# Inverse of the 32x32 diagonal blocks in the second mixer: one partition per block, or four partitions per block and a transposition on TensorE

## The chip, the cores and the metric

The kernel runs on one core of a Trainium2 chip. The metric is device time in microseconds (us). Before the change the median of three runs is 1167.81 us, from 1162.26 to 1176.41.

## The reference: what is computed

Two blocks of a language model run one after the other on 256 tokens of width 1024. The first has a stick-breaking attention, an RWKV-7 recurrence and a feed-forward layer. The second has a token mixer (a gated delta rule and HGRN2, four heads of 128 each) and a mixture of 64 experts. This case is about one line of the gated delta rule:

```python
L = jnp.where(strict, jnp.einsum('bhncd,bhnsd->bhncs', kb, kc) * decay, 0.0)
sol = lax.linalg.triangular_solve(L + jnp.eye(CHUNK, dtype=L.dtype), rhs,
                                  left_side=True, lower=True, unit_diagonal=True)
```

The kernel works on chunks of 128 tokens and not of 64, so there are 4 heads times 2 chunks = 8 systems of 128x128, all unit lower triangular. It forms the inverse of I + L for each. What the later products take is N, the transposed inverse.

## The kernel before

The kernel is one stream of instructions for each engine. Its parts are Python generators that are stepped in the order of a string. For the second mixer this string is `MIXER` ('kkkffkfkkfkfffffffkfqkkqqqqqqqqddghh...'): k is `proj_gdn` (keys, gates, the matrices L and the inverse), f is `proj_hgrn`, q is `proj_qv` (the query and value projections with a convolution and a SiLU), g is `proj_gates2`, d is `gdn` (the products that read N) and h is `hgrn`. The string gives priorities only: a planner in the framework, with its own costs for each instruction, then orders the instructions of each engine, so instructions of f, q, g and h stand between those of the inverse. On the chip each engine's queue runs in that order.

**Projections.** Weights arrive as units of 8 tiles of 128x128 (512 KB). `unit` loads `raw` from DRAM by the SP queue (L274), ScalarE rounds it to `whi` (L324), and VectorE, or for a fixed list of units GpSimd, takes the rest `wlo` = raw - whi (L325). There are three buffers each of raw, whi and wlo. Each tile is then multiplied in three TensorE matmuls (L330, L331, L332, or L352, L357, L358 for the gates): whi by the high part of the input, whi by its low part, wlo by the high part.

**The inverse** (`inverse`, called in the second mixer for 8 systems, and in the first block for 16 systems with `extra`, before the change the same code). Each 128x128 system has four 32x32 blocks on its diagonal, so 8 systems give 32 small blocks. L goes to DRAM (L421) and comes back with one block in each partition, 32 partitions in use (L424, four DMAs). `base_inverse` inverts all of them at once by forward substitution: for each of 31 columns j one VectorE multiplication (L403) and one subtraction (L404) on a rectangle of 31-j rows by j+1 columns. ScalarE writes the transposed copy (L405). Both forms go to DRAM (L435, two DMAs) and are read back to where they stand on the diagonal: the transposed form into N (L439, four DMAs), the untransposed form of the first three blocks into Mc (L442, three DMAs). Two levels of small TensorE products (`mm` at L413, evacuated at L454, L459, L464, L473 and L477) then fill 64x64 and 128x128. `gdn` reads N.

Around the inverse on VectorE stand the convolutions of q (L1145), its SiLU (L1150), the gates (L1314) and the levels of HGRN2 (L1435, L1436, L1438, L1447); on GpSimd its share of L325, L1439 and copies (L1425); on TensorE the products of HGRN2 (L1441) and the transpositions (`tr`, L389). After the mixer come the output projection, the router, a sort of the experts, and the experts, whose weights stream in at full DMA rate.

Of the kernel before, what the change touches and what calls it, by code (L numbers as in the profile page):

```python
# [10 lines left out]
F32 = mybir.dt.float32  # L11
# [3 lines left out]
AF = mybir.ActivationFunctionType  # L15
OP = mybir.AluOpType
# [193 lines left out]
class Ker:  # L210
# [193 lines left out]
            nc.vector.tensor_tensor(M[:, c:, :c], M[:, c:, :c], u, op=OP.subtract)  # L404
        nc.scalar.activation(MT[:P], M.rearrange("p a b -> p b a"), AF.Copy)  # L405

    def inverse(self, L, ns, N, tag, extra=None):

        nc = self.nc
        mm = lambda out, l, r: nc.tensor.matmul(out, l, r, start=True, stop=True)  # L413
        ne = 4 * ns + (8 if extra else 0)
        nc.gpsimd.memset(N, 0.0)
        work = self.alloc("gate", [4, 1024])
        Mc = work[:, 0, :ns * 64].rearrange("p (a b) -> p a b", b=64)
        nc.gpsimd.memset(Mc, 0.0)
        inst, A0, A1 = (work[:, i].rearrange("p (a b) -> p a b", b=32) for i in (1, 2, 3))
        dl = self.dram.tile([128, ns, 128], F32, name=f"dl{ns}")  # L420
        nc.sync.dma_start(dl, L)  # L421
        for k in range(4):
            q = slice(32 * k, 32 * k + 32)
            nc.sync.dma_start(inst[k * ns:(k + 1) * ns], dl[q, :, q].rearrange("t s c -> s t c"))  # L424
        if extra:
            dm = self.dram.tile([128, 2, 32], F32, name="dm")
            nc.sync.dma_start(dm, extra[0])
            for g in range(2):
                o = 4 * ns + 4 * g
                nc.sync.dma_start(inst[o:o + 4], dm[:, g].rearrange("(i t) c -> i t c", i=4))  # L430
        A = A0, A1
        self.base_inverse(inst, A0, A1, ne)
        da = self.dram.tile([2, ne, 32, 32], F32, name=f"da{ns}")
        for x in range(2):
            nc.sync.dma_start(da[x], A[x][:ne])  # L435
        for k in range(4):
            q = slice(32 * k, 32 * k + 32)
            s = slice(k * ns, (k + 1) * ns)
            nc.sync.dma_start(N[q, :, q], da[1, s].rearrange("s t c -> t s c"))  # L439
            if k < 3:  # L440
                o = 32 * (k % 2)
                nc.sync.dma_start(Mc[q, :, o:o + 32], da[0, s].rearrange("s t c -> t s c"))  # L442
            if extra:
                nc.sync.dma_start(extra[1][q, :, q], da[1, 4 * ns:].rearrange("(g i) t c -> i t g c", g=2)[k])
        yield

        X = work[:, 1, :ns * 64].rearrange("p (a b) -> p a b", b=64)
        half = [(slice(64 * p, 64 * p + 32), slice(64 * p + 32, 64 * p + 64)) for p in range(2)]
        v = lambda p: p.rearrange("p (a b) -> p a b", b=32)[:, :ns]
        px = [v(self.psum(tag)) for _ in range(2)]  # L450
        for p, (f, z) in enumerate(half):
            for s in range(ns):
                mm(px[p][f, s], L[z, s, f], N[z, s, z])
            nc.scalar.activation(X[f, :, :32], px[p][f], AF.Copy)  # L454
        pn = [v(self.psum(tag)) for _ in range(2)]
        for p, (f, z) in enumerate(half):
            for s in range(ns):
                mm(pn[p][f, s], Mc[f, s, :32], X[f, s, :32])
            nc.vector.tensor_scalar(N[f, :, z], pn[p][f], -1.0, None, op0=OP.mult)  # L459
        pm = v(self.psum(tag))  # L460
        f, z = half[0]
        for s in range(ns):
            mm(pm[z, s], X[f, s, :32], Mc[f, s, :32])
        nc.scalar.activation(Mc[z, :, :32], pm[z], AF.Copy, scale=-1.0)  # L464
        yield

        X = work[:, 2, :ns * 64].rearrange("p (a b) -> p a b", b=64)
        f, z = slice(0, 64), slice(64, 128)
        for b in range(0, ns, 8):
            px = self.psum(tag).rearrange("p (a b) -> p a b", b=64)  # L470
            for s in range(8):
                mm(px[f, s], L[z, b + s, f], N[z, b + s, z])
            nc.scalar.activation(X[f, b:b + 8], px[f], AF.Copy)  # L473
            pn = self.psum(tag).rearrange("p (a b) -> p a b", b=64)
            for s in range(8):
                mm(pn[f, s], Mc[f, b + s], X[f, b + s])
            nc.vector.tensor_scalar(N[f, b:b + 8, z], pn[f], -1.0, None, op0=OP.mult)  # L477
# [1714 lines left out]
```

## Time and profile before

| | |
|---|---|
| median of 3 runs | 1167.81 us (1162.26 to 1176.41) |
| the profiled execution, its own time | 1168.17 us |
| its span, first to last instruction | 1166.3 us |
| mean granted clock of TensorE, share of full speed | 0.971 |
| TensorE matmul busy | 1085.4 us (93%) |
| VectorE busy | 682.4 us (59%) |
| ScalarE busy | 436.3 us (37%) |
| GpSimd busy | 243.7 us (21%) |
| DMA, mean over the span | 249 GB/s |

The profiled execution is 0.36 us above the median. Engines in the rows: PE is TensorE's matmuls, PEld its weight loads, DVE is VectorE, ACT is ScalarE, POOL is GpSimd, SP is the engine whose queue issues most DMAs (SPq). A row of the timeline has the start in us, the duration in us, engine, line, operation, output<-inputs, partitions x elements, count, and in brackets the idle time just before with what ended it. The inverse of the second mixer takes from 588.8 us (L goes to DRAM) to about 674 us.

### The profile page before, as it was taken

How to read it: one execution, taken by the hardware profiler on the slowest of the kernel's cores; microseconds unless marked ns; L12 is line 12 of the kernel's file. 1: busy time of each engine (PE TensorE's matmuls, PEld its weight loads, DVE VectorE, ACT ScalarE, POOL GpSimd, SP SyncE). 2: the span in 40 equal slices, each digit the busy share in tenths (PEclk: the TensorE clock that was granted, in tenths of full speed). 3: DMA queues.
4: the chain of work that ended last, by engine and by line, in shares of the span. 5: the costliest groups of instructions: out<-in, count | busy, mean ns of one | idle time of the engine just before them, and what ended most of it. 6: DMA issues, size and time to landing. Idle time of an engine off the chain costs nothing.

```text
span 1166.3 us, 20384 instructions
## 1 busy us (share of the span) xinstructions
PE 1085.4 (93%) x8050; PEld 825.3 (71%) x8050; DVE 682.4 (59%) x1211; ACT 436.3 (37%) x707; POOL 243.7 (21%) x245
## 2 busy tenths in 40 slices
PE   4989899999999999888988999899999999999994
PEld 4889787789989999887988889773454455444441
DVE  5598633356688887878799887612333333333333
ACT  5744433365454444335864635311111111111112
POOL 1251102123321000577462141410000000000000
PEclk9899979999999999999999999799999999999997
DMA  4445511024568988763443405959999999999992
GB/s 171 146 141 178 175 62 38 1 91 163 181 248 288 330 319 326 277 247 136 157 135 126 160 28 187 412 179 373 418 409 418 418 419 419 399 420 418 419 419 115
DMA packets 67496, 290.70 MB, mean 249 GB/s; under 512 B 15984, under 2 KB 17136, under 8 KB 46912
## 3 DMA queue, kind: packets, MB, share of 16 engines
q1 hardware_dynamic: 66528, 287.93, 64.9%
q8 instruction: 66, 1.08, 0.4%
q10 hardware_dynamic: 864, 1.38, 0.3%
q14 instruction: 38, 0.31, 0.1%
HBM read 285.77 MB, written 3.51 MB: 248 GB/s over the span
## 4 chain that ended last, share of the span: by engine, by line
PE 51%; DVE 13%; DMA 9%; issue 4%; ACT 4%; POOL 3%; SPq 0%; DVEq 0%; POOLq 0%; ACTq 0%
PE bank L1892 14%; PE bank L1920 7%; DMA wada<-in_W_ada_dram 5%; PE acc L1789 4%; PE bank L1852 4%; DMA er<-in_E_dram 3%; DVE wlo L325 3%; DVE wada L1098 2%; PE p_b L797 2%; PE p_b L357 2%; PE p_b L358 2%; ACT k L306 2%; PE p_b L352 2%; PE p_b L331 2%; PE p_b L332 2%
## 5 line engine op out<-in xcount | busy, mean ns | idle before, releaser
L324 ACT ACTIVATE whi<-raw 128x1024 fp32r<-128x1024 f32 x168 | 175.4, 1055 | 100.9 <-DMA raw<-in_W_dram 36.9
L325 DVE TENSOR_TENSOR wlo<-raw,whi 128x1024 fp32r<-128x1024 f32 x138 | 179.3, 1305 | 54.9 <-ACT whi L324 50.6
L358 PE MATMUL p_b<-k,wlo 128*128 128x256 f32 x608 | 173.5, 286 | 6.9 <-DVE wlo L325 5.1
L357 PE MATMUL p_b<-k,whi 128*128 128x256 f32 x608 | 173.1, 285 | 2.3 <-DVE k L325 2.3
L352 PE MATMUL p_b<-k,whi 128*128 128x256 f32 x608 | 172.8, 285 | 1.5 <-ACT whi L324 0.7
L332 PE MATMUL p_b<-k,wlo 128*128 128x256 f32 (+2 forms) x496 | 144.1, 295 | 12.9 <-DVE wlo L325 8.9
L330 PE MATMUL p_b<-k,whi 128*128 128x256 f32 (+2 forms) x496 | 146.4, 299 | 6.7 <-ACT k L324 4.1
L331 PE MATMUL p_b<-k,whi 128*128 128x256 f32 (+2 forms) x432 | 126.8, 296 | 1.5 <-DVE k L1122 0.9
L358 PEld LDWEIGHTS p_b<-k,wlo 128*128 128x128 f32 x608 | 115.7, 191 | 11.0 <-DVE wlo L325 6.9
L325 POOL TENSOR_TENSOR wlo<-raw,whi 128x1024 fp32r<-128x1024 f32 x30 | 80.9, 2700 | 191.0 <-ACT whi L324 159.1
L357 PEld LDWEIGHTS p_b<-k,whi 128*128 128x128 f32 x608 | 115.7, 190 | 3.7 <-DVE k L325 2.7
L352 PEld LDWEIGHTS p_b<-k,whi 128*128 128x128 f32 x608 | 115.5, 190 | 3.1 <-ACT whi L324 0.9
L332 PEld LDWEIGHTS p_b<-k,wlo 128*128 128x128 f32 (+1 forms) x496 | 96.4, 196 | 15.6 <-DVE wlo L325 10.9
L330 PEld LDWEIGHTS p_b<-k,whi 128*128 128x128 f32 (+1 forms) x496 | 96.8, 197 | 12.4 <-ACT k L324 5.1
L1892 PE MATMUL bank<-er,x 128*32 128x512 f32 (+2 forms) x464 | 91.9, 611 | 2.7 <-DMA er<-in_E_dram 2.5
L1920 PE MATMUL bank<-er,k 128*32 128x512 f32 (+2 forms) x488 | 90.2, 604 | 2.6 <-DMA er<-in_E_dram 1.4
L1098 DVE SCALAR_TENSOR_TENSOR wada<-wada,crow 128x1024 f32<-128x1024 f32 x48 | 74.9, 1564 | 22.9 <-DMA wada<-in_W_ada_dram 22.8
L1892 PE MATMUL bank<-er,h 128*32 128x512 f32 (+2 forms) x488 | 87.3, 595 | 0.0
L1840 POOL TENSOR_TENSOR k<-k,masks 128x128 f32<-128x128 f32 (+3 forms) x44 | 17.4, 425 | 334.2 <-DVE y L325 309.2
L331 PEld LDWEIGHTS p_b<-k,whi 128*128 128x128 f32 (+1 forms) x432 | 85.5, 199 | 2.2 <-DVE k L1122 1.1
L1897 ACT ACTIVATE k<-bank 128x256 f32<-128x256 f32 x24 | 9.2, 385 | 195.1 <-PE bank L1892 195.1
L1898 DVE SCALAR_TENSOR_TENSOR k<-k,gs,bank 128x256 f32<-128x256 f32 x24 | 11.5, 480 | 101.8 <-ACT k L1897 101.8
(478 smaller groups left out, 2043.8 us busy)
## 6 DMA issues: line engine op xcount, KB each, us to landing
er<-in_E_dram SPq DMA_DIRECT2D x132, 1024.0 KB, 18.0
raw<-in_W_dram SPq DMA_DIRECT2D x168, 512.0 KB, 3.9
wada<-in_W_ada_dram SPq DMA_DIRECT2D x48, 512.0 KB, 5.4
xa<-in_E_dram SPq DMA_DIRECT2D x24, 1024.0 KB, 13.2
xa<-in_Sh_dram SPq DMA_DIRECT2D x2, 1024.0 KB, 9.2
k<-in_xT_dram SPq DMA_DIRECT2D x4, 272.0 KB, 5.0
dl<-x SPq DMA_DIRECT2D x1, 1024.0 KB
x<-in_xT_dram SPq DMA_DIRECT2D x1, 1024.0 KB
```

What stands on the lines that cost most here:

```text
L324: ins = self.nc.scalar.activation(hi, src, AF.Copy)
L325: (engine or self.nc.vector).tensor_tensor(lo, src, hi.bitcast(F32), op=OP.subtract)
L330: mm(out, w[0], x[0], start=start, stop=False)
L331: mm(out, w[0], x[1], start=False, stop=False)
L332: mm(out, w[1], x[0], start=False, stop=stop)
L352: a = mm(p[:, i], w[0], v[0], start=(n == 0), stop=False, **kw)
L357: mm(p[:, i], w[0], v[1], start=False, stop=False, **kw)
L358: mm(p[:, i], w[1], v[0], start=False, stop=last, **kw)
L1098: nc.vector.scalar_tensor_tensor(w, w, 1.0, c, op0=OP.mult, op1=OP.mult, accum_out=self.mod[:, o:o + 1])
L1789: self.nc.tensor.matmul(self.acc[t], w, x, start=t not in self.started, stop=False, skip_group_check=True)
L1892: mm(ph[t], X[:, k, i * 128 + t.start:i * 128 + t.stop], u[:, kk * 512:kk * 512 + 512], start=(k == 0), stop=(k == KD - 1), skip_group_che ...
L1920: nc.tensor.matmul(py[t], q.H[:, k, t], u[:, k * 1024 + c * 512:k * 1024 + c * 512 + 512], start=(k == 0), stop=(k == 1), skip_group_check ...
```

## The change

For the call without `extra` (the second mixer) the blocks are inverted by a new function `by_columns`; the first block keeps the code of before under the name `by_blocks`. A block now goes to four partitions, 128 in all: partition 32c + 8k + s holds block k of system s and solves for columns c, c+4, c+8, ... of its inverse. To load it takes 16 DMAs in place of four, since each block is copied four times. A step j works on 31-j rows by j//4+1 columns. Five small memsets on GpSimd set up the unit columns, in place of two. Only the transposed form goes through DRAM: one DMA out, in runs of 128 B, and four back into N. The three DMAs into Mc are gone; after the `yield`, TensorE transposes all eight 128x128 systems of N and six ScalarE copies take the first three diagonal blocks into Mc. The levels above stay as they are.

```diff
+    def by_columns(self, L, N, Mc, work, tag):
+        nc = self.nc
+        ns = 8
+        b = lambda x, n: x.rearrange("p (a b) -> p a b", b=n)
+        inst, M, MT = b(work[:, 1], 32), b(work[:, 2, :256], 8), b(work[:, 3, :256], 32)
+        u, flat = work[:, 2, 256:512], work[:, 2, :256]
+        nc.gpsimd.memset(flat, 0.0)
+        for c in range(4):
+            nc.gpsimd.memset(flat[32 * c:32 * c + 32, 8 * c::33], 1.0)
+        dl = self.dram.tile([128, ns, 128], F32, name=f"dl{ns}")
+        nc.sync.dma_start(dl, L)
+        for k in range(4):
+            q = slice(32 * k, 32 * k + 32)
+            for c in range(4):
+                o = 32 * c + ns * k
+                nc.sync.dma_start(inst[o:o + ns], dl[q, :, q].rearrange("t s c -> s t c"))
+        for j in range(31):
+            r, c = 31 - j, j // 4 + 1
+            v = u[:, :r * c].rearrange("p (a b) -> p a b", b=c)
+            nc.vector.tensor_tensor(v, inst[:, j + 1:, j:j + 1].to_broadcast([128, r, c]), M[:, j:j + 1, :c].to_broadcast([128, r, c]), op=OP.mult)
+            nc.vector.tensor_tensor(M[:, j + 1:, :c], M[:, j + 1:, :c], v, op=OP.subtract)
+        nc.scalar.activation(MT, M.rearrange("p a b -> p b a"), AF.Copy)
+        da = self.dram.tile([8, 128, 32], F32, name=f"da{ns}")
+        nc.sync.dma_start(da.rearrange("i p t -> p i t"), MT)
+        back = da.rearrange("i (c k s) t -> (i c) k s t", c=4, k=4)
+        for k in range(4):
+            q = slice(32 * k, 32 * k + 32)
+            nc.sync.dma_start(N[q, :, q], back[:, k])
+        yield
+        for h in (0, 4):
+            pt = b(self.psum(tag), 128)
+            for s in range(4):
+                self.tr(pt[:, s], N[:, h + s])
+            for k in range(3):
+                q = slice(32 * k, 32 * k + 32)
+                o = 32 * (k % 2)
+                nc.scalar.activation(Mc[q, h:h + 4, o:o + 32], pt[q, :, q], AF.Copy)
+
...
+    def inverse(self, L, ns, N, tag, extra=None):
...
+        if not extra:
+            yield from self.by_columns(L, N, Mc, work, tag)
+        else:
+            yield from self.by_blocks(L, ns, N, Mc, work, extra)
```

## Rows read from the trace of the kernel before

**Rows 1.** The page, part 2: busy tenths in 40 slices

```profile
PE   4989899999999999888988999899999999999994
...
DVE  5598633356688887878799887612333333333333
```

**Rows 2.** Stretches: length, busy (count) of PE, PEld, DVE, ACT, POOL; PEclk, DMA share, GB/s

```profile
597.00:652.10 55.10, 46.78 (x359) 45.40 (x358) 54.50 (x109) 28.16 (x38) 15.22 (x10) 0.94 0.37 128
600.30:604.20 3.90, 3.84 (x20) 3.84 (x20) 3.66 (x9) 1.68 (x3) 2.81 (x5) 0.57 0.36 134
616.40:622.00 5.60, 5.52 (x32) 5.35 (x32) 5.60 (x10) 1.36 (x2) 2.60 (x1) 0.70 0.54 189
653.20:674.00 20.80, 20.80 (x226) 18.62 (x227) 15.92 (x22) 13.88 (x21) 7.19 (x5) 1.00 0.42 129
674.00:690.00 16.00, 13.79 (x109) 12.33 (x108) 15.06 (x29) 4.29 (x8) 4.37 (x6) 1.00 0.10 34
```

**Rows 3.** Timeline of TensorE: four idle times in 597:653

```profile
600.36 0.38 PE L332 MATMUL p_b<-k,wlo 128*128 128x256 f32 x1 [2.34 <-POOL wlo L325]
...
616.48 0.39 PE L332 MATMUL p_b<-k,wlo 128*128 128x256 f32 x1 [2.49 <-DVE wlo L325]
...
631.73 0.39 PE L332 MATMUL p_b<-k,wlo 128*128 128x256 f32 x1 [1.64 <-POOL wlo L325]
...
648.80 0.38 PE L358 MATMUL p_b<-k,wlo 128*128 128x256 f32 x1 [1.66 <-DVE wlo L325]
```

**Rows 4.** VectorE groups, 597 to 652.1 us: the base inverse

```profile
L404 DVE TENSOR_TENSOR gate<-gate,kt 32x31 f32<-32x31 f32 (+15 forms) x31 | 18.8, 606 | 0.2
...
L403 DVE TENSOR_TENSOR kt<-gate 32x31 f32<-32x31 f32 (+15 forms) x31 | 10.9, 352 | 0.3
```

**Rows 5.** Timelines of VectorE and GpSimd: one overlap, durations by shape

```profile
605.28 2.50 DVE L404 TENSOR_TENSOR gate<-gate,kt 32x156 f32<-32x156 f32 x1
...
604.87 2.75 POOL L325 TENSOR_TENSOR wlo<-raw,whi 128x1024 fp32r<-128x1024 f32 x1 [1.76 <-ACT whi L324]
...
597.34 0.19 DVE L403 TENSOR_TENSOR kt<-gate 32x31 f32<-32x31 f32 x1
...
648.68 0.23 DVE L403 TENSOR_TENSOR kt<-gate 32x87 f32<-32x87 f32 x1
...
623.22 0.40 DVE L403 TENSOR_TENSOR kt<-gate 32x256 f32<-32x256 f32 x1
...
594.54 0.41 DVE L1435 TENSOR_TENSOR h<-h 128x256 f32<-128x256 f32 x1
```

**Rows 6.** SP's queue at the inverse's start, landing of block loads

```profile
591.42 1.54 SPq L424 DMA_DIRECT2D gate<-dl  x4
...
593.05 0.94 SPq L274 DMA_DIRECT2D raw<-in_W_dram  x2
...
DMA to landing us min/median/max: 4.4/4.9/5.1
```

**Rows 7.** Timelines of ScalarE and VectorE: the first later weight splits

```profile
602.80 2.98 ACT L324 ACTIVATE whi<-raw 128x1024 fp32r<-128x1024 f32 x3
...
604.15 1.20 DVE L325 TENSOR_TENSOR wlo<-raw,whi 128x1024 fp32r<-128x1024 f32 x1
```

**Rows 8.** The way back: SP, ScalarE, TensorE; transpositions in 560:735

```profile
652.04 2.81 SPq L435 DMA_DIRECT2D da<-gate  x2
...
652.50 2.01 ACT L405 ACTIVATE gate<-gate 32x1024 f32<-32x1024 f32 x1
...
666.46 0.38 ACT L454 ACTIVATE gate<-p_b 32x256 f32<-32x256 f32 x1
...
661.97 0.69 PE L413 MATMUL p_b<-k,k 32*32 32x32 f32 x16
...
L389 PE MATMUL p_b<-masks,k 128*128 128x128 f32 x26 | 4.2, 280 | 2.1 <-DVE k L1188 0.8 <-DVE k L1337 0.8 <-DVE k L374 0.5
```

**Rows 9.** SP's waits from 690 us: us, times, longest

```profile
SPq L1804 <- DVE masks L1709: 15.4, 1, 15.4
```

More of the change, by code (lines that the diff above doesn't have):

```diff
@@ L405, in base_inverse @@
         nc.scalar.activation(MT[:P], M.rearrange("p a b -> p b a"), AF.Copy)
-    def inverse(self, L, ns, N, tag, extra=None):
+    def by_columns(self, L, N, Mc, work, tag):
         nc = self.nc
[L413 to L418, printed above, removed]
+        ns = 8
[33 more added lines that the diff above has]
+                nc.scalar.activation(Mc[q, h:h + 4, o:o + 32], pt[q, :, q], AF.Copy)
@@ L419, in inverse, with by_blocks @@
+    def by_blocks(self, L, ns, N, Mc, work, extra):
+        nc = self.nc
+        ne = 4 * ns + 8
         inst, A0, A1 = (work[:, i].rearrange("p (a b) -> p a b", b=32) for i in (1, 2, 3))
@@ L424, in inverse @@
             nc.sync.dma_start(inst[k * ns:(k + 1) * ns], dl[q, :, q].rearrange("t s c -> s t c"))
[L425 to L430, printed above, removed]
+        dm = self.dram.tile([128, 2, 32], F32, name="dm")
+        nc.sync.dma_start(dm, extra[0])
+        for g in range(2):
+            o = 4 * ns + 4 * g
+            nc.sync.dma_start(inst[o:o + 4], dm[:, g].rearrange("(i t) c -> i t c", i=4))
         A = A0, A1
@@ L442, in inverse @@
                 nc.sync.dma_start(Mc[q, :, o:o + 32], da[0, s].rearrange("s t c -> t s c"))
-            if extra:
-                nc.sync.dma_start(extra[1][q, :, q], da[1, 4 * ns:].rearrange("(g i) t c -> i t g c", g=2)[k])
+            nc.sync.dma_start(extra[1][q, :, q], da[1, 4 * ns:].rearrange("(g i) t c -> i t g c", g=2)[k])
         yield
+    def inverse(self, L, ns, N, tag, extra=None):
+        nc = self.nc
+        mm = lambda out, l, r: nc.tensor.matmul(out, l, r, start=True, stop=True)
+        nc.gpsimd.memset(N, 0.0)
+        work = self.alloc("gate", [4, 1024])
+        Mc = work[:, 0, :ns * 64].rearrange("p (a b) -> p a b", b=64)
+        nc.gpsimd.memset(Mc, 0.0)
+        if not extra:
+            yield from self.by_columns(L, N, Mc, work, tag)
+        else:
+            yield from self.by_blocks(L, ns, N, Mc, work, extra)
         X = work[:, 1, :ns * 64].rearrange("p (a b) -> p a b", b=64)
```

## The prediction, made before the changed kernel ran

> **What bounds the kernel now.** I read the page first, by slices: TensorE is busy nine tenths or more in most of them, and VectorE reaches its highest shares, eight tenths and more, only in the middle [rows 1]. Then the stretches: from 597 to 652.1 us, the time in which the second mixer's base inverse runs, VectorE is busy for 54.5 of 55.1 us, and TensorE for 46.8 [rows 2]. So here, and only here, VectorE is the full engine and TensorE the one that waits. From 653.2 to 674 us TensorE is busy throughout, and from 674 to 690 us for 13.8 of 16 us [rows 2]. The idle times of TensorE come next: four long ones of 2.34, 2.49, 1.64 and 1.66 us, all for a `wlo` (L325), twice one made on GpSimd [rows 3]. They make 8.1 of the 8.3 us that TensorE stands idle in the stretch. After two of them the granted clock is down: its mean is 0.57 over 3.9 us and 0.70 over 5.6 us [rows 2], between the levels of 2.4 and 1.2 GHz. That costs 3.9 x 0.43 = 1.7 us and 5.6 x 0.30 = 1.7 us. All that TensorE loses beside the inverse is thus 8.3 + 3.4 = 11.7 us, about 1% of the kernel. Nothing that the change does to VectorE there can give back more, unless it also shortens the work after it.
>
> A gain here passes on to the end. The loads of the sorted experts wait 15.4 us for the sort (L1709), which follows the mixer and the router [rows 9], so they move with the mixer's end.
>
> **VectorE, the term that is meant to fall.** L403 and L404 have the same 31 shapes, but take 10.9 and 18.8 us [rows 4]. The 7.9 us between them are not arithmetic: the L404 at 605.28 us takes 2.50 us while GpSimd's L325 runs from 604.87 to 607.62 us [rows 5], and there are four such pairs. Twice 10.9 = 21.8 us is then the plain time of the 62 instructions.
>
> The new 62 instructions work on 8 to 76 elements in a partition, 1560/31 = 50 in the mean, where the old ones had 31 to 256. A row of 31 elements takes 0.19 us, one of 87 0.23 us, one of 256 0.40 us, and 256 elements in 128 partitions take 0.41 us [rows 5], so more partitions cost nothing. At 50 elements I take 0.20 us: 62 x 0.20 = 12.4 us. The ends are 62 x 0.23 = 14.3 us, and 62 x 0.17 = 10.5 us with the line through 31 and 256 drawn on to 8 elements. The number of instructions stays, so most of what is left is the fixed part. Saved: 21.8 - 12.4 = 9.4 us, between 7.5 and 11.3.
>
> Are the 7.9 us of stalls saved too? The rows show a VectorE instruction with two inputs in SBUF that ends when GpSimd's ends [rows 5]; GpSimd keeps the same splits. I leave the stalls where they are: another L404 or an L325 will meet them. The Trainium skill, SBUF — State Buffer, section SBUF: two separate sides, speaks against the change in the same way: the port pair that VectorE and GpSimd share is an exclusive lock, and whoever comes second blocks fully. By that rule the stall stays and 9.4 us is all; without it up to 17.3 us would go.
>
> **What TensorE gets of it.** VectorE then has 54.5 - 9.4 = 45 us of work in the stretch, TensorE needs 46.8 - 3.4 = 43.4 us. The two are nearly even, and the order on VectorE decides. By idle time: the one before 600.36 us, with its slow stretch (2.34 + 1.7), ends with GpSimd's own work and began before the base inverse did at 597.34 us [rows 3, 5]; it gives nothing. The one before 616.48 us comes when little of the 9.4 us has been saved; I take 1.5 of 2.49 us, and half of the 1.7 us behind it. Those before 631.73 and 648.80 us, late in the stretch, I take in full, 1.64 and 1.66 us. Sum: 1.5 + 0.85 + 1.64 + 1.66 = 5.6 us, between 0 and 2.49 + 1.7 + 1.64 + 1.66 = 7.5 us.
>
> **What is added.**
> - TensorE: 8 transpositions. 26 such take 4.2 us busy, 0.16 us each [rows 8], so 1.3 us on an engine that is full after 653 us. Counted whole.
> - SP's queue: 16 block loads for four. Four took 1.54 us [rows 6], 0.385 us each; twelve more are 4.6 us. Two loads of raw weights stand right behind, at 593.05 us, and move to about 597.7 us; with the 4.4 us that a block load takes to land [rows 6] the first is there at 602.1, and ScalarE takes it up at 602.80 us [rows 7]. That is free with 0.7 us to spare; if the cover is gone it is as much as 4.6 us.
> - The base inverse itself then begins 4.6 us later, at 602 us. Before, VectorE did nothing but base inverse from 597.34 us to the L325 at 604.15 us [rows 5, 7], so a late start idles it where nothing else was ready. The instructions that the planner puts ahead of that L325 have to be caught up. From 0 to 4.6 us; I take 0.4, since some 11 instructions of 0.20 us fit between 602 and 604.2 us.
> - The way back: the second DMA out, the 2.0 us of the old transposed copy and three loads go; one DMA out in short runs, eight transpositions and six copies of about 0.38 us [rows 8] come. Before, the first products came at 661.97 us, 9.9 us after the first DMA out at 652.04 us [rows 8], with TensorE busy on gates and HGRN2. With the base inverse over some 20 us earlier, the same cover (projections of q, gates) is there. Taken as 0; without cover it is a wait on TensorE (below). ScalarE's net is 6 x 0.38 + 0.4 - 2.0 = +0.7 us in a stretch where it is busy for 28.2 of 55.1 us [rows 2]: 0.
> - GpSimd's memsets can run long before, while the work tile is free: 0. The levels above the blocks do not change.
>
> **Sum.** -5.6 + 1.3 + 0.4 = -3.9 us against the profiled execution's 1168.17 us, that is 1164.3, say 1164 us. Its span of 1166.3 us has 1.9 us around it that do not move, and it stands 0.36 us above the median of 1167.81 us. About 1%, 11.7 us, is what a measurement of this kernel can tell from no change; the forecast lies well inside.
>
> **Rivals.**
> - *No change* (1167 to 1170 us): VectorE frees time, but the weight splits wait for GpSimd, ScalarE and raw loads all the same, and 1.3 us of transpositions eat the rest. For it: two of the four idle times end with GpSimd's split [rows 3]. Against: VectorE's 54.5 us of 55.1 [rows 2].
> - *More than forecast*: the inverse is complete some 20 us earlier, so `gdn` can start while projections still run, and the mixer's end packs closer. Then all 11.7 us beside the inverse go, and the 16 - 13.8 = 2.2 us idle from 674 to 690 us [rows 2]: 1168.2 - 13.9 + 1.3 = 1155.6 us. This needs GpSimd's early wait to vanish as well, for which I see no reason, save that the planner's order of all engines is new from 590 us on.
> - *Slower*: the block data arrives late, and instructions that need it stand ahead of work that doesn't, in queues that run in order. At the start: 16 loads at the slower landing of 5.1 us [rows 6], with raw loads behind them, put the base inverse at 603 to 605 us; the L325 at 604.15 us [rows 7] stands behind it and goes late by up to 4.6 us, and TensorE with it, plus a slow stretch of 1.7 us. At the way back: the transpositions stand in TensorE's queue before N has landed. N comes after a DMA out and loads, 9.9 us in all before [rows 8]; if the planner allows for half of that, TensorE stands 5 us and 1.7 us slow. 4.6 + 1.7 + 5 + 1.7 + 1.3 = 14.3 us against a gain of about 3: 1179.5 us. It decides from the point where the round trip is over 4 us longer than planned. The Trainium skill, DMA: Bandwidth & Descriptors, section Specifications, asks for transfers of at least 512 B for line rate; the new DMA out has runs of 128 B into DRAM, and no row here shows such a write. By that rule the way back would be longer and this case likelier.
> - *That VectorE's time does not fall* because the fixed part rules: the 31-element row at 0.19 against 0.40 us [rows 5] leaves no room for that; it is in the ends above.
>
> **Chances.** The forecast (1160 to 1167) 0.43; no change 0.22; more than forecast 0.20, of which 0.13 beyond 1%; slower 0.15, of which 0.10 beyond 1%. So faster by over 1%: 0.13; within: 0.77; slower: 0.10. The range takes in the forecast, no change, and most of both outer cases: 1155 to 1176 us.
>
> **What would show it.** Right: L403 and L404's successors at about 0.20 us apiece, 12 to 14 us with fewer or equal stalls of some 2 us; VectorE below nine tenths beside the inverse; the waits of TensorE for L325 after 610 us shorter; SP's queue holding 16 block loads for about 6 us; first products of the upper levels 15 to 25 us earlier. Wrong: TensorE standing in front of L389 with a DMA as the cause, raw loads that land after ScalarE is free, VectorE idle before the first base instruction with L325 behind it, or a mixer whose later part (674 us on) is stretched by what the first part gained.

## The result, and the profile after

The changed kernel takes 1183.72 us in the median of 11 runs (1178.77 to 1192.26), the kernel before, run beside it, 1169.1 us (1162.26 to 1176.41): a ratio of 1.013, with a 95% interval of 1.0103 to 1.0157. It is 1% slower, where I had forecast 1164 us and a small gain. The profiled execution of the changed kernel took 1192.09 us (span 1190.3), near the upper end of its runs, so I don't compare whole spans: 3.5 us of the difference are there before the change begins (the projections' first product is at 593.2 instead of 589.7 us), and 5 us come behind the router. What the edit can touch directly is the stretch between. I take it from the first product of the projections (the row of TensorE with 1.2 us idle for L1286, L1331 in the changed kernel) to the router's first transposition. It grew from 147.6 to 163.1 us, by 15.5 us, as much as the 1.3% of the timed runs (0.013 x 1169 = 15.2 us). Such a stretch is of one execution, so it shows where the time goes, and the timed runs how much it is.

Cut in three, before: projections; from their last product to the output projection's first (gates, inverse, gated DeltaNet, HGRN2: "the middle" from here on); output projection. Columns as in [rows 2].

```profile
589.74:633.17 43.43, 36.37 (x268) 35.19 (x269) 42.55 (x81) 20.99 (x29) 22.34 (x12) 0.92 0.41 138
633.17:702.93 69.76, 65.17 (x579) 59.57 (x578) 62.45 (x119) 39.10 (x59) 17.29 (x17) 1.00 0.28 94
702.93:737.36 34.43, 32.78 (x258) 31.38 (x258) 20.02 (x40) 14.08 (x27) 5.33 (x8) 1.00 0.68 261
```

The same three in the changed kernel:

```profile
593.22:637.30 44.08, 36.30 (x264) 34.97 (x264) 34.93 (x86) 21.46 (x29) 21.17 (x12) 0.88 0.57 144
637.30:722.26 84.96, 71.22 (x590) 65.49 (x590) 60.23 (x115) 39.48 (x65) 16.65 (x17) 0.94 0.25 74
722.26:756.34 34.08, 32.42 (x255) 31.18 (x255) 19.79 (x39) 14.01 (x27) 5.31 (x8) 1.00 0.70 268
```

Read the second rows: the middle is 15.2 us longer (84.96 - 69.76). TensorE's idle time in it went from 69.76 - 65.17 = 4.6 to 84.96 - 71.22 = 13.7 us, so 9.1 us are waits; its busy time rose by 6.0 us, at a granted clock of 0.94 for 1.00 and with the eight transpositions added. The projections gained nothing: 44.08 for 43.43 us, although VectorE does 7.6 us less there (34.93 for 42.55).

**VectorE did get its time back.** The steps of the base inverse, as groups of the changed kernel between 600 and 650 us; they answer to [rows 4]:

```profile
L428 DVE TENSOR_TENSOR gate<-gate 128x60 f32<-128x60 f32 (+24 forms) x31 | 10.8, 349 | 8.3 <-DMA gate<-dl 7.9
L429 DVE TENSOR_TENSOR gate<-gate 128x60 f32<-128x60 f32 (+24 forms) x31 | 8.7, 281 | 0.5
```

10.8 + 8.7 = 19.5 us for the 29.7 us of L403 and L404: 10.2 us saved, 9.4 forecast. VectorE's timeline shows single steps and a stall; GpSimd's shows what is beside the stall:

```profile
611.70 0.21 DVE L428 TENSOR_TENSOR gate<-gate 128x50 f32<-128x50 f32 x1
611.94 0.21 DVE L429 TENSOR_TENSOR gate<-gate 128x50 f32<-128x50 f32 x1
...
613.20 2.38 DVE L428 TENSOR_TENSOR gate<-gate 128x48 f32<-128x48 f32 x1
```

```profile
612.32 3.19 POOL L325 TENSOR_TENSOR wlo<-raw,whi 128x1024 fp32r<-128x1024 f32 x1 [5.78 <-ACT whi L324]
```

A step of 50 elements takes 0.21 us, and the one that meets GpSimd's split takes 2.38 us: the stall stayed, as forecast. There are three such steps, 7.2 us together, where the kernel before had four, 9.2 us; the other 59 steps take 12.3 us, 0.21 us each. (By the exclusive lock of the Trainium skill, SBUF — State Buffer, section SBUF: two separate sides, this had to be so; the trace agrees, 2.38 for 0.21 us.)

**The start.** SP's queue, VectorE, ScalarE and TensorE of the changed kernel where the base inverse begins; they answer to [rows 3, 6, 7]:

```profile
592.28 0.33 SPq L419 DMA_DIRECT2D dl<-k  x1
594.91 9.53 SPq L424 DMA_DIRECT2D gate<-dl  x16
604.54 1.30 SPq L274 DMA_DIRECT2D raw<-in_W_dram  x3
```

```profile
608.76 0.20 DVE L428 TENSOR_TENSOR gate<-gate 128x31 f32<-128x31 f32 x1 [7.86 <-DMA gate<-dl]
...
609.90 1.06 ACT L324 ACTIVATE whi<-raw 128x1024 fp32r<-128x1024 f32 x1 [3.13 <-DMA raw<-in_W_dram]
...
611.01 0.58 PE L330 MATMUL p_b<-k,whi 128*128 128x256 f32 x1 [2.98 <-ACT whi L324]
...
613.34 0.58 PE L332 MATMUL p_b<-k,wlo 128*128 128x256 f32 x1 [1.11 <-DVE wlo L325]
```

Of these 16 loads, the shortest, the median and the longest on SP, in ns:

```profile
L424 SPq DMA_DIRECT2D gate<-dl x16: 308/369/2006, 594.9 to 603.7; - x16
```

The 16 loads take SP 9.53 us, not the 6.2 us that 16 x 0.385 makes. The base inverse begins 608.76 - 593.22 = 15.5 us behind the projections' first product; before, it was 597.34 - 589.74 = 7.6 us, so it is 7.9 us later, not 4.6. Raw weights stand behind them and are issued at 604.54 us, 12.3 us after the first DMA out; before, with the DMA out at 588.80 us, it was 593.05 - 588.80 = 4.3 us. ScalarE waits for them, TensorE for ScalarE.

**The way back.** SP, then TensorE's first products of the upper levels, as [rows 8]:

```profile
648.14 0.43 SPq L432 DMA_DIRECT2D da<-gate  x1
653.45 1.97 SPq L436 DMA_DIRECT2D k<-da  x4
```

```profile
656.10 0.69 PE L482 MATMUL p_b<-k,k 32*32 32x32 f32 x16 [1.07 <-DMA k<-da]
```

The round trip is 656.10 - 648.14 = 8.0 us, shorter than the 9.9 us before, and TensorE waits 1.07 us at it. But the inverse is not complete some 20 us earlier: counted from the projections' first product, this row is at 656.10 - 593.22 = 62.9 us, before at 661.97 - 589.74 = 72.2 us, 9.3 us earlier. The short steps stand one by one between other work in VectorE's queue, and the last of them ends at 646.2 us. SP stands 5.3 us between the DMA out and the first load. (The Trainium skill, DMA: Bandwidth & Descriptors, section Specifications, asks for 512 B a piece; this DMA out has pieces of 128 B. That it is the size, and not the raw weights that move at the same time, no run here shows; with the longer pieces of the kernel before, such a DMA out landed in 2.4 us at most there, and in up to 5.1 us in e11_before_gates_first.)

**The middle.** This is TensorE's order behind the projections, counted from its instructions: g gates, h HGRN2, i the inverse's upper levels, t transpositions, n norms, d gated DeltaNet, | router weights, m output projection (broken off after 90 of its products). A product counts once here; the trace has two rows for each of h, i, n and d, one for each of the others. First before, then changed:

```
g14 h4 g26 h4 g18 h4 g60 h4 g18 h4 g38 i8 g4 i8 g14 i8 h4 i16 t4 i8 n1 h1 i8 n1 h3 t8 h8 d4 t4 d12 h2 d4 t4 h4 t4 d1
h2 d4 h3 d7 h4 d8 h9 d2 h4 t4 h4 | m3 h8 m18 h4 m69

g48 h16 g39 i8 g9 t8 h1 i8 h4 i24 h3 i8 g6 i8 n2 g8 t4 g26 d4 g13 t4 g2 d4 g6 d8 g9 d4 t4 g4 t4 g1 d1 g5 d4 g6 d7 g6
d8 g4 h4 t4 h4 t4 h8 d2 h8 | h4 | h20 t4 h1 m3 h7 m18 h4 m69
```

Before, the gates are through before gated DeltaNet begins, and HGRN2 and gated DeltaNet take turns. In the changed kernel the last 90 products of the gates come behind gated DeltaNet's norms, 56 of them between its products, HGRN2 has no turn between 663.4 and 694.3 us, and its products then stand almost alone. TensorE there, in the changed kernel:

```profile
694.32 1.05 PE L1486 MATMUL p_b<-h 128*128 128x128 f32 x8
...
697.64 1.13 PE L1490 MATMUL p_b<-h,h 128*128 128x128 f32 x8 [1.83 <-DVE k L1359]
...
705.31 3.36 PE L1486 MATMUL p_b<-h 128*128 128x128 f32 x16 [1.88 <-POOL h L1484]
...
712.59 1.13 PE L1486 MATMUL p_b<-h 128*128 128x128 f32 x8 [0.97 <-DVE h L1483]
715.18 2.11 PE L1486 MATMUL p_b<-h 128*128 128x128 f32 x16 [1.47 <-DVE h L1483]
```

and the corresponding place before, where nothing waits:

```profile
694.78 2.18 PE L1441 MATMUL p_b<-h 128*128 128x128 f32 x18
696.81 1.98 PE L1381 MATMUL p_b<-k,ones 128*128 128x512 f32 x4
698.63 1.05 PE L1445 MATMUL p_b<-h,h 128*128 128x128 f32 x8
```

No level of HGRN2 reads another's product, but each product (L1486, before L1441) needs operands that VectorE, ScalarE and GpSimd make one behind the other (L1480, L1481, the exponential L306, L1483, L1484). With other products between, these steps are hidden; without them TensorE waits. From 694.3 to 722.3 us it waits 8.4 of 28 us. The other 5.3 of its 13.7 us of waits are about as much as the 4.6 us before.

The other part of the 15 us is busy time. Two more waits, and the transpositions:

```profile
639.43 0.35 PE L352 MATMUL p_b<-k,whi 128*128 128x256 f32 x1 [2.14 <-DVE gate L429]
...
657.87 1.04 PE L389 MATMUL p_b<-masks,k 128*128 128x128 f32 x8
...
674.78 1.83 PE L1381 MATMUL p_b<-k,k 128*128 128x128 f32 x8 [1.82 <-DVE k L1205]
```

Behind these two waits, and behind the 1.88 us at 705.31, the granted clock is down. The three spells, then 2 us out of each:

```profile
641.00:645.00 4.00, 4.00 (x23) 4.00 (x23) 4.00 (x13) 1.06 (x1) 0.00 (x0) 0.58 0.65 171
674.00:679.00 5.00, 4.22 (x23) 4.22 (x24) 3.85 (x5) 0.61 (x2) 0.00 (x0) 0.66 0.61 185
705.30:710.00 4.70, 4.69 (x27) 4.69 (x28) 4.04 (x8) 1.89 (x3) 1.54 (x2) 0.64 0.00 0
```

```profile
642.00:644.00 2.00, 2.00 (x11) 2.00 (x11) 2.00 (x7) 0.12 (x1) 0.00 (x0) 0.50 0.84 266
...
676.00:678.00 2.00, 2.00 (x11) 2.00 (x11) 1.88 (x3) 0.00 (x0) 0.00 (x0) 0.50 0.46 123
...
706.00:708.00 2.00, 2.00 (x11) 2.00 (x11) 2.00 (x4) 1.13 (x3) 0.84 (x2) 0.50 0.00 0
```

0.50 is the level of 1.2 GHz, and TensorE does 11 products in 2 us where at 1.00 it does 20 (651 to 653 us). By the means the spells cost 4.00 x 0.42 + 5.00 x 0.34 + 4.70 x 0.36 = 5.1 us, an estimate; with the 1.04 us of the transpositions that is about the 6.0 us of busy time. Before, the middle has no such stretch. Only the third spell stands behind a wait of HGRN2; the first stands behind a wait for a late step of the inverse on VectorE, the second behind the one at gated DeltaNet's first product. So HGRN2's bare end makes 8.4 + 1.7 = 10.1 of the 15.2 us directly.

### The profile page after: what moved, and what is told of

It is laid out like the page before. It is cut to its first block, busy times and chain, and to the rows that moved or that the text cites. A ratio compares the mean times of both kernels' runs of the same rounds, so it can differ in the third digit from the quotient of the medians.

```text
span 1190.3 us, 20429 instructions
## 1 busy us (share of the span) xinstructions
PE 1093.1 (92%) x8058; PEld 834.4 (70%) x8058; DVE 674.5 (57%) x1211; ACT 437.1 (37%) x713; POOL 240.8 (20%) x248
## 4 chain that ended last, share of the span: by engine, by line
PE 51%; DVE 12%; DMA 10%; ACT 3%; POOL 3%; issue 3%; SPq 1%; POOLq 0%; ACTq 0%; DVEq 0%
PE bank L1937 13%; PE bank L1965 7%; DMA wada<-in_W_ada_dram 5%; PE acc L1834 4%; PE bank L1897 4%; DMA er<-in_E_dram 3%; DVE wlo L325 3%; DVE wada L1143 2%; PE p_b L357 2%; PE p_b L358 2%; PE p_b L352 2%; PE p_b L842 2%; ACT k L306 1%; PE bank L1798 1%; PE p_b L332 1%
## 5 line engine op out<-in xcount | busy, mean ns | idle before, releaser
L325 DVE TENSOR_TENSOR wlo<-raw,whi 128x1024 fp32r<-128x1024 f32 x138 | 176.2, 1283 | 58.7 <-ACT whi L324 54.8
L358 PE MATMUL p_b<-k,wlo 128*128 128x256 f32 x608 | 176.0, 290 | 6.5 <-DVE wlo L325 4.7
L352 PE MATMUL p_b<-k,whi 128*128 128x256 f32 x608 | 175.1, 289 | 3.6 <-DVE gate L429 2.1
L357 PE MATMUL p_b<-k,whi 128*128 128x256 f32 x608 | 175.2, 288 | 2.4 <-DVE k L325 2.4
L332 PE MATMUL p_b<-k,wlo 128*128 128x256 f32 (+2 forms) x496 | 144.3, 295 | 10.9 <-DVE wlo L325 7.6
L358 PEld LDWEIGHTS p_b<-k,wlo 128*128 128x128 f32 x608 | 117.9, 194 | 10.2 <-DVE wlo L325 5.9
L352 PEld LDWEIGHTS p_b<-k,whi 128*128 128x128 f32 x608 | 117.3, 193 | 5.7 <-issue 3.5
L357 PEld LDWEIGHTS p_b<-k,whi 128*128 128x128 f32 x608 | 117.8, 194 | 3.9 <-DVE k L325 2.8
L1143 DVE SCALAR_TENSOR_TENSOR wada<-wada,crow 128x1024 f32<-128x1024 f32 x48 | 76.5, 1595 | 21.6 <-DMA wada<-in_W_ada_dram 21.6
```

The source lines that it names most:

```text
L325: (engine or self.nc.vector).tensor_tensor(lo, src, hi.bitcast(F32), op=OP.subtract)
L332: mm(out, w[1], x[0], start=False, stop=stop)
L352: a = mm(p[:, i], w[0], v[0], start=(n == 0), stop=False, **kw)
L357: mm(p[:, i], w[0], v[1], start=False, stop=False, **kw)
L358: mm(p[:, i], w[1], v[0], start=False, stop=last, **kw)
L1143: nc.vector.scalar_tensor_tensor(w, w, 1.0, c, op0=OP.mult, op1=OP.mult, accum_out=self.mod[:, o:o + 1])
```

## The experiments

Theory A: the loss is the order that the planner makes of gates, gated DeltaNet and HGRN2 behind the projections. Theory B, the rival: 16 loads and the way back hold SP's queue, and what needs the data comes late. The stretch is that of the profiled run, one execution of each kernel, with its three parts and TensorE's idle time in the middle:

| run | median us | ratio (95%) | stretch | projections, middle, output | idle in the middle |
|---|---|---|---|---|---|
| before | 1169.1 | 1 | 147.6 | 43.4, 69.8, 34.4 | 4.6 |
| changed | 1183.7 | 1.0130 (1.0103 to 1.0157) | 163.1 | 44.1, 85.0, 34.1 | 13.7 |
| e1_steps | 2774.0, not compared | | 160.3 | 41.7, 84.5, 34.1 | 11.6 |
| e2_turn | 1172.8 | 1.0013 (0.9991 to 1.0035) | 151.3 | 45.8, 71.0, 34.5 | 5.1 |
| e3_pack | 1185.1 | 1.0134 (1.0057 to 1.0211) | 162.8 | 42.8, 85.9, 34.1 | 11.3 |
| e4_order | 1181.7 | 1.0099 (1.0076 to 1.0122) | 156.1 | 43.7, 79.1, 33.3 | 11.8 |
| e5_h_late | 1184.6 | 1.0108 (1.0064 to 1.0152) | 162.3 | 43.4, 84.8, 34.1 | 10.3 |
| e6_h_first | 1191.5 | 1.0178 (1.0120 to 1.0236) | 166.1 | 43.8, 89.6, 32.7 | 15.6 |
| e7_before_h_first | 1187.2 | 1.0135 (1.0081 to 1.0189) | 165.2 | 46.0, 88.3, 31.0 | 14.5 |
| e8_pack_h_first | 1183.1 | 1.0110 (1.0075 to 1.0145) | 163.8 | 43.2, 89.1, 31.5 | 14.3 |
| e9_gates_first | 1179.1 | 1.0157 (1.0044 to 1.0270) | 155.7 | 44.7, 76.5, 34.5 | 8.4 |
| e10_pack_gates_first | 1176.2 | 1.0120 (1.0014 to 1.0226) | 156.9 | 43.0, 79.4, 34.5 | 8.0 |
| e11_before_gates_first | 1176.6 | 1.0140 (1.0025 to 1.0254) | 157.8 | 43.5, 79.3, 35.0 | 10.9 |
| e12_h_in_mix | 1184.6 | 1.0200 (1.0086 to 1.0314) | 161.1 | 42.5, 66.0, 52.6 | 7.1 |

**e1_steps**: the kernel before with the small steps alone; its four loads and its way back stay.

```
-            r, c = B - 1 - j, j + 1
+            r, c = B - 1 - j, j + 1 if P > 32 else j // 4 + 1
...
```

> The kernel before, with the second mixer's 62 base-inverse instructions cut to the sizes of the change (j//4+1 columns, still 32 partitions; the other columns of the blocks are left unsolved); loads, way back and everything else as before. VectorE's relief alone. The planner's order on TensorE is the changed kernel's here: gates spread among the products of gdn, and some 30 products of HGRN2 in a row ahead of the output projection. Theory A (the order: a base inverse that the planner expects earlier pulls gdn ahead and leaves HGRN2's chain bare): 8 to 14 us slower than before, idle times of 1 to 2 us between HGRN2's products. Theory B (the block loads and the way back hold SP's queue): these are as before, so 4 to 9 us faster than before.

Its blocks are left unsolved in part, so the router gets other values and the experts other loads; I read it up to the router. The middle is 84.5 us, as in the changed kernel, without one new DMA. Three parts, by stretches:

```profile
591.77:633.51 41.74, 35.09 (x264) 34.08 (x264) 38.50 (x90) 21.25 (x29) 20.37 (x12) 0.92 0.45 152
633.51:718.04 84.53, 72.96 (x582) 65.95 (x582) 58.85 (x112) 39.46 (x59) 18.62 (x17) 0.90 0.22 73
718.04:752.11 34.07, 32.41 (x254) 31.16 (x254) 19.80 (x39) 14.02 (x27) 5.33 (x8) 1.00 0.72 285
```

and HGRN2's waits at the end are those of the changed kernel, to the hundredth:

```profile
693.07 1.13 PE L1445 MATMUL p_b<-h,h 128*128 128x128 f32 x8 [1.83 <-DVE k L1314]
...
700.73 3.68 PE L1441 MATMUL p_b<-h 128*128 128x128 f32 x16 [1.88 <-POOL h L1439]
708.01 1.13 PE L1441 MATMUL p_b<-h 128*128 128x128 f32 x8 [0.97 <-DVE h L1438]
710.60 3.29 PE L1441 MATMUL p_b<-h 128*128 128x128 f32 x16 [1.47 <-DVE h L1438]
```

TensorE's order there is that of the changed kernel too: again the last 90 products of the gates come behind gated DeltaNet's norms, and HGRN2's stand at the end. So shorter steps are enough for the loss in the middle; theory B is not needed for it. The shares differ: 7.0 us more idle time than before, and 7.8 us more busy time at a clock of 0.90. In the projections this run is 1.7 us shorter than before. The kernel before had 43.4 to 46.0 us there under other orders (e5, e7, e11), so 1 to 2 us in this part can't be told from what an order does.

**e2_turn**: the kernel before with the transposed form made by TensorE (8 transpositions, 6 copies), and its second DMA out and three loads gone.

```
...
-            if k < 3:
+            if k < 3 and extra:
...
+        for h in () if extra else (0, 4):
+            ...
+                self.tr(pt[:, s], N[:, h + s])
```

> The kernel before, with Mc made by eight TensorE transpositions and six ScalarE copies and not by three loads, and one DMA out in place of two. The other part alone; the planner's order on TensorE stays that of before. Theory A: within 2 us of before, from -2 to +2. Theory B: faster by 1 to 3 us, since SP's queue has four DMAs less; both say that this part is not the loss.

1.0013, no change that can be measured. The middle is 71.0 us, 1.3 us more than before, as much as the term that I counted for the transpositions (0.7 us of it is busy time, the rest waits); the order stays close to that of before. TensorE has no wait of over 0.3 us for the way back. (Its projections are 2.4 us longer in this profile; I have not followed that up.)

**e3_pack**: the changed kernel with the diagonal blocks packed in DRAM.

```
...
+        dl = self.dram.tile([32, 32, 32], F32, name=f"dl{ns}")
         for k in range(4):
...
+            nc.sync.dma_start(dl[ns * k:ns * k + ns].rearrange("s t c -> t s c"), L[q, :, q])
+        for c in range(4):
+            nc.sync.dma_start(inst[32 * c:32 * c + 32], dl)
```

> The changed kernel, with the blocks packed on their way out (four DMAs to DRAM in runs of 128 B) and read back by four DMAs of 32 partitions x 4 KB in place of 16. SP's queue is held for some 3 us and not 9.5. The planner's order keeps the bare chain of HGRN2. Theory A: still 8 to 13 us slower than before, though VectorE's wait for the blocks falls from 7.9 us to under 4. Theory B: back to before or up to 5 us faster than before.

SP's queue is free at once, as its rows show:

```profile
592.79 1.80 SPq L421 DMA_DIRECT2D dl<-k  x4
596.81 1.71 SPq L423 DMA_DIRECT2D gate<-dl  x4
598.56 2.50 SPq L274 DMA_DIRECT2D raw<-in_W_dram  x3
```

Yet the time is 1185.05 us and the middle 85.9 us. So the 16 loads are not the reason of the loss in the middle, and theory B falls for them. The projections are 1.3 us shorter than in the changed kernel: about that much the late raw weights cost. They don't get lower because of the next wait, now at VectorE, where the split stands behind steps of the inverse:

```profile
612.79 0.58 PE L332 MATMUL p_b<-k,wlo 128*128 128x256 f32 x1 [5.13 <-DVE wlo L325]
```

**e4_order**: the changed kernel with a tail of MIXER that gives HGRN2 earlier turns (the tail is what follows the first 31 letters, which place the projections).

```
-MIXER = '...ddghhfdhhgdhhgghhhhhhdhhhghh'
+MIXER = '...hhghhghhghhgddhhfdhhdhhhhdhg'
```

> The changed kernel, with another string MIXER after its first 31 letters ('hhghhghhghhgddhhfdhhdhhhhdhg': gates and HGRN2 ahead of gdn); all instructions as in the changed kernel, 16 loads too. The planner then puts three quarters of the gates ahead of gdn and HGRN2's products between them. Theory A: the 13 us come back, 1160 to 1172 us, and the idle times of TensorE between HGRN2's products go. Theory B: the loads are the same, so 1178 to 1186 us as in the changed kernel.

The stretch is 7 us shorter than in the changed kernel, the middle 79.1 us: in the profile nearly half of the loss came back. The time did not follow so far: 1181.7 us, 10 us above what was expected, and 1.0099 for 1.0130, with intervals that overlap. The gates were through by 679 us, and behind them gated DeltaNet and HGRN2 wait for VectorE by turns. Of the 11.8 us that TensorE idles here, 3.5 us come before that, two waits of 1.25 and 2.30 us (635.1 and 642.1 us) for late steps of the inverse on VectorE. Its granted clock was 1.00 over the whole middle, though single waits were as long as 2.36 us:

```profile
632.95:712.05 79.10, 67.29 (x606) 61.91 (x604) 60.87 (x122) 40.31 (x66) 16.68 (x17) 1.00 0.24 80
```

**e5_h_late**: the kernel before, nothing of its inverse touched, with a tail that puts the gates first and HGRN2 last.

```
-MIXER = '...ddghhfdhhgdhhgghhhhhhdhhhghh'
+MIXER = '...fddgdgdggdghhhhhhhhhhhhhhhhh'
```

> The kernel before, its inverse untouched; only the string MIXER, by which the mixers' parts take turns, has a new tail ('fddgdgdggdg' and 17 h), so that the 192 products of the output gates come first and HGRN2's last 28 products stand with nothing beside them in front of the output projection, as in the changed kernel. Theory A (the loss of the changed kernel is the order of gates, gated DeltaNet and HGRN2 behind the projections): the stretch from the end of the projections to the output projection grows from 69.3 us by 6 to 15, the kernel is 6 to 15 us slower (1175 to 1184) although no instruction of the inverse differs, with waits of TensorE of 0.5 to 2 us between HGRN2's last products. Theory B (16 loads, the way back): no loss, 1167 to 1172, since the order of the mixers is not what costs.

1184.56 us: an order alone costs the kernel before what the whole change costs. The projections are the same to the hundredth (43.43 us), the middle is 84.75 us:

```profile
588.24:631.67 43.43, 36.31 (x268) 35.13 (x269) 42.55 (x81) 20.91 (x29) 22.27 (x12) 0.92 0.42 138
631.67:716.42 84.75, 74.42 (x580) 65.96 (x579) 64.32 (x120) 39.38 (x59) 19.09 (x17) 0.90 0.24 77
```

HGRN2 stands alone at the end, with waits that the changed kernel has too (1.47, 0.42, 0.98 us there):

```profile
709.35 2.11 PE L1441 MATMUL p_b<-h 128*128 128x128 f32 x16 [1.35 <-DVE h L1438]
...
712.81 1.16 PE L1441 MATMUL p_b<-h 128*128 128x128 f32 x8 [0.42 <-POOL h L1439]
...
715.83 0.46 PE L1473 MATMUL p_b<-h,h 128*128 128x128 f32 x2 [0.97 <-DVE h L1447]
```

Its shares are others than in the changed kernel: 5.7 us more idle time than before, and 9.3 us more busy time, since the clock fell for about 16 us behind the waits and the small products around 660 us:

```profile
664.00:672.00 8.00, 7.96 (x82) 7.33 (x82) 4.66 (x10) 1.38 (x3) 1.72 (x2) 0.51 0.16 59
672.00:680.00 8.00, 8.00 (x39) 5.00 (x39) 2.09 (x3) 1.85 (x3) 0.00 (x0) 0.50 0.00 0
```

So a bad order costs about 15 us here, but this one is not the changed kernel's: its gates are all ahead of the inverse, and more than half of its loss is 16 us at half the clock, which the changed kernel does not have. It shows that an order can cost as much, not by which waits the changed kernel's does.

**e6_h_first, e7_before_h_first, e8_pack_h_first**: one tail, HGRN2 first, in the changed kernel, in the kernel before and with packed blocks.

```
+MIXER = '...hhhhhhhhhhhhhhhhhddgfdgdggdg'
```

> The changed kernel with another tail of MIXER: 17 h first, then d and g, so that HGRN2's levels come ahead of gated DeltaNet's and half of the gates are left to fill gated DeltaNet's waits. Theory A: the stretch behind the projections falls from 85.0 us to 68 to 74, and the kernel to 1164 to 1173. Theory B: 1180 to 1187, as the changed kernel.

> The control of e6_h_first: the kernel before with the same tail of MIXER. Theory A: within 6 us of the kernel before (its own order was good already); what e6_h_first is ahead or behind this one is then what the inverse by columns is worth when the order is the same: 0 to 6 us faster by the forecast's sum. Theory B: e6_h_first is 10 to 18 us slower than this one.

> The changed kernel with the blocks packed into one piece of DRAM (4 writes and 4 loads in place of 1 and 16) and the tail of MIXER of e6_h_first. Theory A: 1160 to 1172, within 4 us of e6_h_first, since the loads were shown to cost nothing. Theory B: nothing below 1178.

All three missed: I had taken this order for a good one, and its middle is the longest, 88 to 90 us, at 1183 to 1192 us. HGRN2 stood alone ahead of gated DeltaNet instead of behind it, which moves the bare chain and doesn't fill it. What e6 and e7 still tell: with the same tail no gain of the inverse by columns can be seen (a stretch of 166.1 against 165.2 us), and the kernel before loses 17 us by a string alone (1187.15 against 1170.23 us beside it; 1.4% by the ratio). With packed blocks (e8) the median is 8.4 us below e6's, where I had expected at most 4; the stretch is only 2.3 us shorter, and the intervals of the two overlap. What the rest of the 8.4 us is, no run shows.

**e9_gates_first, e10_pack_gates_first, e11_before_gates_first**: one tail in which gates and HGRN2 take turns, then HGRN2 and gated DeltaNet.

```
+MIXER = '...hghghghhghfhghddhhdhhdhhdhhh'
```

> The changed kernel with a third tail of MIXER ('hghghhghhfhghddhhdhhdhhdh' and so on): gates and HGRN2's levels take turns ahead of gated DeltaNet, and behind it HGRN2 and gated DeltaNet take turns, so that HGRN2 has ten products left when gated DeltaNet ends, as in the kernel before. Theory A (order): the stretch behind the projections is 68 to 76 us (before 69.3, changed 85.0), the kernel 1163 to 1174. If it stays over 80 us although HGRN2 doesn't stand alone at the end, theory A names the wrong piece of the order, and gates spread behind gated DeltaNet's first products aren't what costs.

> As e9_gates_first, with the blocks packed in DRAM (4 writes, 4 loads). Theory A: within 4 us of e9_gates_first; the 8 us by which the raw weights were issued later in the changed kernel come back only where VectorE's splits don't stand behind the steps of the inverse: 1160 to 1172. Theory B: 5 to 10 us below e9_gates_first.

> The control of e9: the kernel before with the same tail. Theory A: its own order was of this kind already, 1164 to 1175; e9 less this run is what the inverse by columns is worth when the order behind it is alike: by the forecast's sum -4 us, by what e6 and e7 showed +4.

In the profile the changed kernel's middle gains 8.5 us: 76.5 us, with fillers between HGRN2's last products and one wait of 0.60 us there; 68 to 76 us were expected. The median is 4.6 us lower (1179.09 for 1183.72), but the two did not run beside each other, and by the ratios to what ran beside each (1.0157 for 1.0130) no gain can be told. All three times lie above what was expected. By the stretch e9 is 2.1 us ahead of the kernel before with the same tail (155.7 against 157.8 us); by the medians it is 2.5 us behind, less than the 12 us over which the four runs of each spread. The tail does not make the same order of the two: HGRN2 waits 5.45 us at 654.5 us in e11 alone. Packed blocks make it 1176.2 us, level with e11 (1176.6). None of them reaches the kernel before with its own tail.

**e12_h_in_mix**: the changed kernel with gates first and HGRN2's last levels beside the output projection.

```
+MIXER = '...ggggddhhfdhhdhhhhhhhhdhhhhhg'
```

> The changed kernel with a tail that puts the gates first and lets HGRN2's last levels fall beside the output projection's first half, which needs gated DeltaNet alone: TensorE then has filler where HGRN2 waits. Theory A: 1160 to 1175, and no row of HGRN2's last products with a wait of over 1 us in front of it; if the output projection's second half waits for HGRN2 instead, the gain is given back there and the time is 1175 to 1190.

The middle ends 19 us earlier, but the output projection takes 52.6 instead of 34.1 us, as HGRN2's last products now stand in it and its second half waits for them (12.4 us more busy and 6.1 us more idle time): 1184.6 us. The gain is given back there, the second branch of the expectation.

## Why the prediction was wrong

By its own steps:

- *VectorE, -9.4 us*: right in the sum, 10.2 us, and partly by luck. The new steps are as forecast, 62 of 0.21 us with the stalls taken off, 13 us for 12.4. But the 21.8 us taken as the plain time of the old ones was too much: besides the four long stalls, four steps at 600.4 to 602.6 us took 0.66 to 0.69 us beside GpSimd's L1439, where their size takes about 0.25. By my estimate some 7 of the 10.2 us are plain time and some 3 are stalls that I had left where they were.
- *What TensorE gets of it, -5.6 us*: wrong in size. In the projections I had counted 1.5 + 0.85 + 1.64 = 4.0 us of it; the shorter steps alone gave 1.7 us there (e1_steps). In the changed kernel the first wait stayed, as forecast (2.39 us at 603.85), the second is gone and the third is down to 0.90 us (635.85); but the late start brought two new ones, 2.98 us for `whi` at 611.01 and 1.11 us for `wlo` at 613.34. The fourth, 1.66 us in the gates, became one of 2.14 us at 639.43, for VectorE still.
- *The transpositions, +1.3 us*: about right; their row has 1.04 us, and e2_turn's middle is 1.3 us longer.
- *The late start, +0.4 us*: too small. SP needed 9.53 us for the 16 loads, the base inverse began 7.9 us later and not 4.6, and the projections are 44.1 us against 41.7 us in e1_steps, which has four loads: 2.3 us. Four loads of packed blocks (e3_pack) give 1.3 us of that back; the other 1.0 us no run takes apart. With -1.7 us the 2.3 us make the +0.65 us measured.
- *The way back, 0*: nearly right; 8.0 for 9.9 us, and 1.07 us of TensorE's time. Its premise was not: the inverse is complete 9.3 us earlier, not some 20.
- *Where it failed*: the sum ends at 652.1 us. It has no term for the part behind it, where I wrote "The levels above the blocks do not change" and took the cover of gates and HGRN2 as given. That cover is not a property of the kernel but a choice of the planner, which places every product anew when a duration changes. In the changed kernel gated DeltaNet's products come before the gates are through, and HGRN2, last in MIXER, is left over. The term that was 0 measures +15.2 us. e1_steps shows that shorter steps alone bring about this order and the loss, e3_pack that the 16 loads have no part in it. That it is the order and not the short steps themselves rests on e4_order and e9_gates_first, the changed kernel's instructions in other orders, with middles of 79.1 and 76.5 us for 85.0, and on e5_h_late, where an order alone costs the kernel before as much. No order that I tried gave the changed kernel the 69.8 us of before, so that order makes the whole 15.2 us is not shown. That it is the planner's view of when gated DeltaNet becomes ready that turned the order is argued from the two orders, not shown.

Of the rivals, *slower* came nearest with 1179.5 us, but by another mechanism: the start cost 2.3 us and the round trip 1.07, and the rest of the loss is neither's. *More than forecast* named the very event, an earlier gated DeltaNet, and drew the wrong sign from it: I thought of the earlier start as packing the end closer, and did not ask what it would push out of the way. The last sign that I listed as wrong, a later part stretched by what the first part gained, comes nearest to what happened, though the first part gained nothing in the end.

What stays open: what the inverse by columns is worth in the order of before. The planner's order is new with every edit, and I found no tail that gives it that one. With alike tails the stretches of the two kernels are within 2.1 us of each other, either way.

## What to carry to other kernels

Where a planner orders the engines from durations, a cheaper instruction is also a new order: price the stretch behind the edit by asking which chain becomes ready earlier, what filler it will take, and which chain is then left alone. Before the price of an edit is discussed, give the old kernel the new order, or the new kernel several orders: here one string moved the kernel before by up to 17 us, and with the same string the edit moved the stretch by about 2. A count of the products that stand next to each other at the end of each chain told more here than the busy shares.

## What the runs showed of the hardware that I had not expected

- Sixteen loads of 8 partitions each, issued one behind the other, took SP 9.53 us, 0.60 us each, where four in a row took 0.385 us each [rows 6]. They are not alike: the median is 0.37 us, as before, and one of the last five took 2.0 us.
- Waits of TensorE of about 2 us were followed by some 2 us at 0.50 of the clock in the changed kernel (at 642, 676 and 706 us), yet the 1.83 us at 697.64 in the same kernel and waits of 2.30 and 2.36 us in e4_order were not, and in e5_h_late a run of waits of 0.5 to 1.5 us with 32x32 products between them was followed by 16 us at 0.50. The longest wait alone doesn't tell what the clock will cost.
